# Attention's row maximum: four transposing products and a copy replaced by three DMAs through DRAM

## The chip, the cores and the metric

The kernel runs on one core of a Trainium2 chip. The metric is the device time of one execution in microseconds (us). Three executions of the kernel before took 2077.51, 2079.65 and 2083.77 us, so the median is 2079.65 us. A fourth execution was taken by the profiler; it took 2078.25 us, and from its first to its last instruction (its span) 2076.6 us.

## What is computed

One layer of a hybrid encoder is applied with the same weights to two groups of rows: 2048 rows (`x_prompt`) and 512 rows (`x_sample`), each 1024 wide. Every layer has a softmax attention with 8 query heads over 2 key heads, a gated linear attention in both directions, an output projection, and a gated embedding. What matters here is the softmax:

```python
def one_block(q_blk):
    s = jnp.einsum('bkgqd,btkd->bkgqt', q_blk, k).astype(jnp.float32) * scale
    p = jax.nn.softmax(s, axis=-1)
    return jnp.einsum('bkgqt,btkd->bkgqd', p.astype(v.dtype), v)
```

The queries and keys are scaled so that scores are large: a softmax needs each row's maximum taken off before the exponential.

## The kernel before

`build` calls four stages. `stage1` makes the projections and writes q, k, v and the normalised input to DRAM as fp16 pairs (a high half and a low half). `stage2` does the linear attention. `stage3` does the softmax attention and the gates, and `stage4` the output projection and the embedding. The change is in `stage3`.

`stage3` works through 40 items, in the order of the list `items`. An item is one query head over a chunk of 512 rows. The chunks 0 to 3 are the prompt's; each of their items has 16 tiles of 128 keys. Chunk 4 is the sample's; its items have 4 tiles. So there are 32 long items and 8 short ones. They are counted from 0 here: item 8 is the first head of chunk 1, item 39 the last of all.

For each item there are two passes over the keys:

- **The maxima** (`maxima`). For each block of 128 queries and each group of 512 keys, TensorE makes a product of the high halves (`px`, L809), and VectorE reduces it to one maximum per query (`mx`, L815). A last reduction gives `m`, four numbers on each of 128 partitions. L823 and L824 write -m/4096 as two fp16 numbers, `mt`, 128 x 4 x 2. Then four small products with the identity matrix (L827) turn these onto two partitions of a PSUM tile `pn`, and a copy on ScalarE (L828) puts them as rows 64 and 65 under q's low half, the tile `qb`.
- **The head** (`head`). For each key tile, two products add up the scores: L863 with the high half of q (`qa`), and L864 with `qb`, whose 66 rows are the 64 of q's low half and the two of the maximum. The key tile `kb` holds 4096 in its rows 64 and 65, so that L864 takes the maximum off. ScalarE takes the exponential (L865) and rounds it to fp16 (`phi`, L872); VectorE makes the rest (`plo`, L874). The products L844, L848 and L852 add up the output and the sum.

The maxima of an item are made while the head before it runs: `head` calls `pull` after each exponential, and `pull` advances several generators, among them `all_maxima` by the numbers in `steps`. The list `ahead` says how many steps of the next item's maxima are already taken when a head begins: five for most, six to eighteen near the short items. Other generators run beside it in the same way: `all_gates` (L765 loads x, L769 loads weights, L775 multiplies, L786 loads the linear attention's output), `all_sums` (`normalise`) and `all_stores` (L800 writes the mixed result).

The PSUM pool `ps_x` has two buffers. The maxima's `px`, the `pn` of L827 and the `pn` of `normalise` share them, by one tag.

A scheduler decides the final order of each engine's instructions from the dependencies and priorities, at compile time. At run time each engine runs its own list strictly in order and waits on semaphores. All the DMAs spoken of here are issued by SyncE (SP in the profile), from one such list too: a DMA that waits holds up every DMA behind it. `load_q` (L757, L758) fills `qa` and the first 64 rows of `qb` from DRAM, several items ahead (four buffers of each).

Of the kernel before, what the change touches and what calls it, by code (L numbers as in the profile page):

```python
# [9 lines left out]
F32 = mybir.dt.float32  # L10
F32R = mybir.dt.float32r
F16 = mybir.dt.float16
# [8 lines left out]
P = 128  # L21
# [21 lines left out]
    "wg": [2, 4, P, 2, 8, P],  # L43
    "qs": [NCH, 4, P, 512],
    "og": [NCH, P, 4, 512],
    "mx": [NCH, P, 2, 8, 512],
}

# [663 lines left out]
def stage3(net, s, fin=iter(()), top=None, tail=None):  # L712
    nc, tc, d = net.nc, net.tc, net.d
    with ExitStack() as ctx:
# [88 lines left out]
        def maxima(idx, c, h, q):  # L803
            ks = keys(c)
            n = len(ks)
            mx = net.sm.tile([P, 4, n], F32, name=f"mx{n}")
            def product(ti, b):
                ps = ps_x.tile([P, 512], F32, name="px", tag="px")
                nc.tensor.matmul(ps, lhsT=q[0][:, b * P:(b + 1) * P], rhs=ks[ti][0][:, h // 4],  # L809
                                 start=True, stop=True)  # L810
                return ps

            for b in range(4):
                for i in range(n):
                    nc.vector.tensor_reduce(mx[:, b, i:i + 1], product(i, b), axis=AX.X, op=ALU.max)  # L815
                    yield
            if n > 1:
                m = net.sm.tile([P, 4], F32, name="m")
                nc.vector.tensor_reduce(m, mx, axis=AX.X, op=ALU.max)
            else:  # L820
                m = mx[:, :, 0]
            mt = net.sm.tile([P, 4, 2], F16, name="mt")
            nc.vector.tensor_scalar(mt[:, :, 0], m, -1.0 / M_SCALE, None, ALU.mult)  # L823
            nc.vector.scalar_tensor_tensor(mt[:, :, 1], m, -1.0 / M_SCALE, mt[:, :, 0], ALU.mult, ALU.subtract)  # L824
            ps = ps_n_tile()
            for b in range(4):
                nc.tensor.matmul(ps[0:2, b * P:(b + 1) * P], lhsT=mt[:, b], rhs=net.identh, start=True, stop=True)  # L827
            nc.scalar.copy(q[1][64:66], ps[0:2])  # L828

        def head(ks, h, q, ou, pull, last):  # L830
            kv = h // 4
# [378 lines left out]
def build(tc, d):  # L1210
    with ExitStack() as ctx:
        dram = ctx.enter_context(tc.tile_pool(name="scratch", bufs=1, space=DRAM))
        s = {n: [dram.tile(shape[1:], F16 if n in ("xt", "qt", "kt", "vs", "wg") else F32, name=f"scr_{n}{i}") for i in range(shape[0])]
             for n, shape in SCRATCH.items()}
        net = Net(tc, d, ctx)
        top = ctx.enter_context(ExitStack())
# [25 lines left out]
```

## Time and profile before

| what | value |
| --- | --- |
| median of three executions | 2079.65 us (2077.51 to 2083.77) |
| the profiled execution | 2078.25 us |
| its span | 2076.6 us |
| TensorE (PE) busy | 1982.3 us, 95% |
| VectorE (DVE) busy | 1359.3 us, 65% |
| ScalarE (ACT) busy | 1219.1 us, 59% |
| DMA queue of SP: share of 16 engines | 36.7% |
| share of the chain that ended last | PE 73%, DVE 11%, ACT 9%, DMA 3% |

The granted TensorE clock was 0.986 of full speed in the mean. `stage3` runs from about 600 to 1530 us. A busy time is a sum over instructions; TensorE's products overlap one another, so that one of them shows 380 ns and the next starts about 215 ns after it. Idle time of an engine matters only where another engine waits for it.

### The profile page before, as it was taken

To read this page: it belongs to the slowest core of one execution; us is meant where nothing else is said; L and a number is where in the kernel's file an instruction comes from. 1 tells how busy PE (TensorE), PEld (TensorE's weight loads), DVE (VectorE), ACT (ScalarE), POOL (GpSimd) and SP (SyncE) were. 2 spreads that over 40 slices of the span, in tenths; PEclk is the share of its full clock that TensorE was granted. 3 is DMA by queue.
4 is the path that set the end of the run, shared out by engine and by line. 5 is a ranking of instruction groups with operands and counts; after the bars stand their busy time and mean duration, and the time that the engine had idled before them with its cause. 6 is when DMAs were issued, how large, how long until landed. Compare 5 with 4: busy or idle time off the path is not lost.

```text
span 2076.6 us, 29930 instructions
## 1 busy us (share of the span) xinstructions
PE 1982.3 (95%) x11176; PEld 1221.5 (59%) x11176; DVE 1359.3 (65%) x2295; ACT 1219.1 (59%) x2136; POOL 357.0 (17%) x293
## 2 busy tenths in 40 slices
PE   8999998999879999999999999999989999999998
PEld 6888886556654333333333333333347888888886
DVE  7557655566678889899989988988973222222223
ACT  6645443555559788788878878878873222222222
POOL 2444441000330011011011011100110111111111
PEclk9999999999999999999999999999999999999999
DMA  7745945355775123322213212311235222222220
GB/s 238 221 118 134 222 108 139 112 175 149 219 233 161 49 69 110 92 76 87 66 72 101 96 59 72 109 41 54 69 116 159 86 87 87 86 87 86 82 66 34
DMA packets 253666, 229.81 MB, mean 111 GB/s; under 512 B 99472, under 2 KB 191472, under 8 KB 253520
## 3 DMA queue, kind: packets, MB, share of 16 engines
q1 hardware_dynamic: 253376, 227.37, 36.7%
q8 instruction: 88, 1.44, 0.3%
q0 software_dynamic: 144, 0.52, 0.1%
q14 instruction: 58, 0.48, 0.1%
HBM read 151.89 MB, written 75.96 MB: 110 GB/s over the span
## 4 chain that ended last, share of the span: by engine, by line
PE 73%; DVE 11%; ACT 9%; DMA 3%; issue 3%; POOL 1%; SPq 0%; DVEq 0%; POOLq 0%; ACTq 0%
PE pm L112 37%; PE pg L775 7%; PE po L852 5%; ACT p L865 4%; PE px L809 4%; PE pss L863 3%; DVE plo L874 3%; PE pss L864 3%; PE po L844 3%; PE pp L112 3%; ACT phi L872 2%; DVE mx L815 2%; PE pz L848 2%; DMA scr_ga<-a 1%; PE pt L1127 1%
## 5 line engine op out<-in xcount | busy, mean ns | idle before, releaser
L865 ACT ACTIVATE p<-pss,lnp,qk_scale 128x512 f32<-128x512 f32 x544 | 406.1, 781 | 102.1 <-PE pss L864 89.3
L815 DVE TENSOR_REDUCE mx<-px 128x1 f32<-128x512 f32 x544 | 355.7, 681 | 60.1 <-PE px L809 58.1
L874 DVE TENSOR_TENSOR plo<-p,phi 128x1024 f16<-128x1024 f32 x272 | 341.4, 1257 | 30.0 <-ACT phi L872 27.5
L872 ACT CAST phi<-p 128x1024 f16<-128x1024 f32 x270 | 283.2, 1049 | 5.3 <-PE po L852 0.8
L775 PE MATMUL pg<-xt,wg 128*128 128x512 f16 x960 | 284.3, 378 | 1.4 <-DVE g L780 1.3
L863 PE MATMUL pss<-qa,ka 128*128 128x512 f16 x544 | 206.0, 379 | 10.5 <-ACT p L865 9.4
L809 PE MATMUL px<-ka,qa 128*128 128x512 f16 x544 | 201.0, 381 | 15.7 <-DVE mx L815 9.7
L864 PE MATMUL pss<-qb,kb 66*128 66x512 f16 x544 | 206.0, 382 | 0.3 <-ACT qb L828 0.3
L775 PEld LDWEIGHTS <-wg 128*128 128x128 f16 x960 | 92.9, 97 | 121.7 <-issue 14.8
L1175 DVE SCALAR_TENSOR_TENSOR th<-th,pp 128x512 f32<-128x512 f32 (+1 forms) x41 | 27.7, 676 | 190.0 <-ACT th L1174 190.0
L852 PE MATMUL po<-phi,v 128*128 128x512 f16 x544 | 142.6, 385 | 0.0
L1128 ACT CAST hT<-pt 128x512 fp32r<-128x512 f32 x40 | 23.5, 587 | 170.7 <-PE pt L1127 170.7
L112 PE MATMUL pm<-xt,whl 128*128 128x512 f16 x480 | 107.7, 384 | 1.9 <-ACT l L492 1.9
L112 PE MATMUL pm<-wq_h,xt 128*128 128x512 f32 x320 | 103.9, 405 | 4.5 <-ACT xt L237 4.0
L1174 ACT ACTIVATE th<-pm,rh 128x512 f32<-128x512 f32 (+1 forms) x41 | 27.8, 679 | 134.1 <-PE pm L112 134.1
L898 POOL TENSOR_TENSOR ou<-ou,rs 128x512 f32<-128x512 f32 x20 | 38.2, 1910 | 378.0 <-DVE rs L896 378.0
L112 PE MATMUL pm<-wpg0h,hT 128*128 128x512 f32 x320 | 101.1, 396 | 0.2 <-DVE hT L1129 0.2
L112 PE MATMUL pm<-wo1h,mx 128*128 128x512 f32 x320 | 100.7, 396 | 0.0
L112 PE MATMUL pm<-wo0h,mx 128*128 128x512 f32 x320 | 100.5, 395 | 0.0
L864 PEld LDWEIGHTS <-kb 66*128 66x128 f16 x544 | 52.8, 97 | 79.6 <-issue 24.6
L112 PE MATMUL pm<-wl_h,xt 128*128 128x512 f32 x320 | 99.6, 392 | 0.0
L112 PE MATMUL pm<-wpg1h,hT 128*128 128x512 f32 (+1 forms) x336 | 99.4, 379 | 0.0
(270 smaller groups left out, 3855.6 us busy)
## 6 DMA issues: line engine op xcount, KB each, us to landing
wg<-scr_wg SPq DMA_DIRECT2D x40, 512.0 KB
scr_mx<-hl SPq DMA_DIRECT2D x40, 512.0 KB
mx<-scr_mx SPq DMA_DIRECT2D x20, 1024.0 KB
x<-x_prompt SPq DMA_DIRECT2D x27, 512.0 KB
scr_xt<-xh SPq DMA_DIRECT2D x20, 512.0 KB
xt<-scr_xt SPq DMA_DIRECT2D x20, 512.0 KB
xt<-scr_xt SPq DMA_DIRECT2D x40, 256.0 KB
wstage<-w_in SPq DMA_DIRECT2D x32, 256.0 KB
```

Of the source, the lines that this page charges most:

```text
L112: self.nc.tensor.matmul(out, lhsT=a[k], rhs=b[k], start=first and i == 0, stop=last and i == n - 1)
L775: nc.tensor.matmul(ps, lhsT=w[:, wi, k], rhs=xi, start=i == 0, stop=i == 23)
L809: nc.tensor.matmul(ps, lhsT=q[0][:, b * P:(b + 1) * P], rhs=ks[ti][0][:, h // 4], start=True, stop=True)
L815: nc.vector.tensor_reduce(mx[:, b, i:i + 1], product(i, b), axis=AX.X, op=ALU.max)
L844: nc.tensor.matmul(po[r:r + 32], lhsT=ks[t // 4][2][:, t % 4 + i, kv, g * 32:g * 32 + 32], rhs=lo[:, i], start=t == 2, stop=False)
L848: nc.tensor.matmul(pz[i * 32:i * 32 + 32], lhsT=ones, rhs=(lo, hi)[i // 2][:, i % 2], start=t == 2, stop=t + 4 == n)
L852: e = nc.tensor.matmul(po, lhsT=ks[t // 4][2][:, t % 4 + i, kv], rhs=hi[:, i], start=False, stop=t + i + 1 == n)
L863: nc.tensor.matmul(ps, lhsT=ka[:, kv, cs], rhs=q[0], start=True, stop=False)
L864: nc.tensor.matmul(ps, lhsT=kb[0:66, kv, cs], rhs=q[1][0:66], start=False, stop=True)
L865: e = nc.scalar.activation(p[:, i], ps, AF.Exp, bias=net.lnp, scale=net.qk_scale)
L872: nc.scalar.copy(hi, p)
L874: nc.vector.tensor_tensor(lo, p, hi, ALU.subtract)
```

## The change

`mt` no longer goes through TensorE and ScalarE. SP writes it to DRAM, in a new scratch array `mt` of 40 x 128 x 4 x 2 fp16, one part for each item. Two more DMAs read it back, one for each of the two fp16 halves, straight into rows 64 and 65 of `qb`. Each of these moves 512 single fp16 numbers: from DRAM every eighth number for a block of queries, onto one partition in a row. The four products, the tile `pn` in `maxima` and the copy are gone.

```diff
     "og": [NCH, P, 4, 512],
+    "mt": [40, P, 4, 2],
     "mx": [NCH, P, 2, 8, 512],
...
             nc.vector.scalar_tensor_tensor(mt[:, :, 1], m, -1.0 / M_SCALE, mt[:, :, 0], ALU.mult, ALU.subtract)
-            ps = ps_n_tile()
-            for b in range(4):
-                nc.tensor.matmul(ps[0:2, b * P:(b + 1) * P], lhsT=mt[:, b], rhs=net.identh, start=True, stop=True)
-            nc.scalar.copy(q[1][64:66], ps[0:2])
+            nc.sync.dma_start(out=s["mt"][idx], in_=mt)
+            for l in range(2):
+                nc.sync.dma_start(out=q[1][64 + l:65 + l].rearrange("l (b p) -> l b p", b=4),
+                                  in_=s["mt"][idx][:, :, l:l + 1].rearrange("p b l -> l b p"))
...
-        s = {n: [dram.tile(shape[1:], F16 if n in ("xt", "qt", "kt", "vs", "wg") else F32, name=f"scr_{n}{i}") for i in range(shape[0])]
+        s = {n: [dram.tile(shape[1:], F16 if n in ("xt", "qt", "kt", "vs", "wg", "mt") else F32, name=f"scr_{n}{i}") for i in range(shape[0])]
```

The first added line moves every later line number up by one: what the kernel before has at L864, the changed one has at L865.

The scheduler orders the lists anew. On SP, around the maxima of item 8, there stood before:

```order
L765 DMA xt_9139<-scr_xt_58 128x2x512
L769 DMA wg_9329<-scr_wg_92 128x2048
L757 DMA qa<-scr_qt_66 128x1x512
L758 DMA qb_9385<-scr_qt_66 64x512
L800 DMA scr_mx_104<-hl 256x1x512
L769 DMA wg_9540<-scr_wg_92 128x2048
```

Now there stand:

```order
L766 DMA xt_9152<-scr_xt_58 128x2x512
L770 DMA wg_9339<-scr_wg_92 128x2048
L826 DMA scr_mt_112<-mt 128x8
L758 DMA qa<-scr_qt_66 128x1x512
L759 DMA qb_9392<-scr_qt_66 64x512
L828 DMA qb_8706<-scr_mt_112 1x512x1 x2
L801 DMA scr_mx_144<-hl 256x1x512
L770 DMA wg_9544<-scr_wg_92 128x2048
```

The write of `mt` (L826) and its two reads (L828) came in, with the q load of a later item between them; what stood there before kept its order.

On PE, at the start of item 39, the last head, there stood before:

```order
L827 LDWEIGHTS mt
L827 MATMUL pn<-identh,mt 2x128
L863 LDWEIGHTS ka
L863 MATMUL pss<-qa,ka 128x512
L864 LDWEIGHTS kb
L864 MATMUL pss<-qb_16516,kb 128x512
```

Now there stand:

```order
L853 LDWEIGHTS v
L853 MATMUL po_16526<-phi,v 128x512
L853 LDWEIGHTS v
L853 MATMUL po_16526<-phi,v 128x512
L865 LDWEIGHTS kb
L865 MATMUL pss<-qb_16439,kb 128x512
```

The first product that reads the two rows (`pss<-qb`) moved behind the last output products of the head before it; the products with `mt` are gone.

## Rows read from the trace of the kernel before

**Rows 1.** The page: its first line, and the chain that ended last, by engine.
```profile
span 2076.6 us, 29930 instructions
PE 73%; DVE 11%; ACT 9%; DMA 3%; issue 3%; POOL 1%; SPq 0%; DVEq 0%; POOLq 0%; ACTq 0%
```

**Rows 2.** Busy time in windows: stretch, its us, busy us (instructions) by engine, clock, DMA.
```profile
600.00:1530.00 930.00, 897.68 (x5618) 364.60 (x5619) 823.58 (x1129) 778.61 (x1078) 107.72 (x67) 0.99 0.26 87
```

**Rows 3.** Groups by line, 600 to 1530 us: count | busy us, mean ns | idle before.
```profile
L827 PE MATMUL pn<-identh,mt 128*2 128x128 f16 x156 | 15.0, 218 | 2.7 <-DVE mt L824 2.7
L828 ACT CAST qb<-pn 2x512 f16<-2x512 f32 x39 | 22.4, 573 | 19.8 <-PE pn L827 19.2
```

**Rows 4.** The chain from 1100 to 1160 us: start us, us, what.
```profile
1102.21 0.87 PE pg L775 x4
1103.08 0.55 PE po L844 x8
1103.63 0.43 PE pz L848 x8
```

**Rows 5.** Timeline of PE around item 8's maxima: start us, us, line, operation.
```profile
819.30 0.38 PE L809 MATMUL px<-ka,qa 128*128 128x512 f16 x1
...
820.82 0.38 PE L863 MATMUL pss<-qa,ka 128*128 128x512 f16 x1
821.12 0.38 PE L827 MATMUL pn<-identh,mt 128*2 128x128 f16 x4
821.44 0.39 PE L809 MATMUL px<-ka,qa 128*128 128x512 f16 x1
...
823.35 0.38 PE L864 MATMUL pss<-qb,kb 66*128 66x512 f16 x1
```

**Rows 6.** Timeline of DVE, the same item.
```profile
820.85 0.17 DVE L824 SCALAR_TENSOR_TENSOR mt<-m,mt 128x4 f16<-128x4 f32 x1
```

**Rows 7.** The tile mt: who waited for it (us, times).
```profile
  PE pn L827: 3.9, 6
```

**Rows 8.** Timelines of PE and DVE at item 39, the last.
```profile
1504.92 0.38 PE L809 MATMUL px<-ka,qa 128*128 128x512 f16 x1
...
1511.41 0.81 PE L864 MATMUL pss<-qb,kb 66*128 66x512 f16 x3 [0.34 <-ACT qb L828]
...
1510.16 0.15 DVE L824 SCALAR_TENSOR_TENSOR mt<-m,mt 128x4 f16<-128x4 f32 x1
```

**Rows 9.** Timelines: a store and the DMA that waits for its landing, twice.
```profile
1592.42 1.01 SPq L1188 DMA_DIRECT2D y_prompt<-x  x2
1595.18 0.34 SPq L1057 DMA_DIRECT2D x<-x_prompt  x1
...
922.55 0.56 SPq L800 DMA_DIRECT2D scr_mx<-hl  x1
925.67 0.32 SPq L786 DMA_DIRECT2D hl<-scr_og  x1
```

**Rows 10.** Timelines: a load and the instruction that waits for it, twice.
```profile
0.81 0.45 SPq L93 DMA_DIRECT2D mixn<-mix_norm  x1
3.28 0.17 DVE L132 TENSOR_SCALAR mix<-mixn 128x8 f32<-128x8 f32 x1 [2.25 <-DMA mixn<-mix_norm]
...
593.12 0.55 SPq L757 DMA_DIRECT2D qa<-scr_qt  x1
600.04 0.61 PE L809 MATMUL px<-ka,qa 128*128 128x512 f16 x1 [2.01 <-DMA qa<-scr_qt]
```

**Rows 11.** Waits, 600 to 1530 us: who for whom, us in total, times, longest.
```profile
ACT p L865 <- PE pss L864: 89.3, 94, 4.2
DVE mx L815 <- PE px L809: 56.3, 85, 2.0
PE pss L863 <- ACT p L865: 9.2, 18, 1.7
PE px L809 <- DVE mx L815: 7.6, 16, 1.1
PE po L844 <- DVE plo L874: 7.2, 17, 0.9
```

**Rows 12.** The DMA queue's own waits, 640 to 1530 us.
```profile
SPq L769 <- PE pg L775: 196.1, 20, 17.4
```

## The prediction

> **What bounds the kernel now.** I read the chain that ended last first: TensorE holds 73% of it [rows 1]. All that changes lies in the softmax stage, so I then read the windows there: in the 930 us from 600 to 1530 us PE was busy 897.68 us, DVE 823.58 and ACT 778.61, at 0.99 of the clock and with 0.26 of the DMA engines' time in use [rows 2]. PE binds, but DVE is close behind (89%), and the three work in small steps on each other's results. The waits say in which direction: ACT waited 89.3 us for the score products and DVE 56.3 us for the maxima's products, while PE's larger waits on ACT and DVE sum to 24 us (9.2 + 7.6 + 7.2) [rows 11]. So a microsecond of PE's list is worth nearly a microsecond, and one of ACT's little.
>
> **What is removed.** On PE, 40 groups of four products. Around item 8 the last product before the group starts at 820.82 us and the first after it at 821.44 [rows 5]; without the group the second would start one product later, about 0.215 us (four of them take 0.87 [rows 4]). The group costs 0.62 - 0.215 = 0.405 us, and 40 of them 16.2 us. To this comes what PE waited for `mt` at these products, 3.9 us in 6 waits [rows 7]. Together 20.1 us, all on PE's list. On ACT, a copy of 573 ns and a wait for it, 22.4 + 19.8 us for 39 of the 40 [rows 3]. ACT waits for PE anyway, so I take nothing for it; if ACT's lateness is what holds the products L863 [rows 11], some 5 us could come from there. The maxima also get back a buffer of `ps_x`; that can't be worth more than the 7.6 us that PE waited for a free one [rows 11], and I take nothing.
>
> **What is added.** Three DMAs for each item, 120 in all, on SP's list, and a wait on PE: the first product on `qb` of a head can't start until both rows have landed. Behind that product stands all of PE's list, so the wait stops the gates and the next maxima too. Its size is the length of the chain from `mt` to the rows, less the work that PE still has in front of that product.
>
> **The chain.** The write first. No row shows a 2 KB store; two stores of 256 KB, the second issued about 0.5 us after 1592.42, had landed at 1595.18, so some 2.2 us for that one; a 512 KB store in this stage took 925.67 - 922.55 = 3.1 us [rows 9]. I take 2.2, since ours is smaller than both. The two reads then: the nearest row in kind is the load of `mixn`, which moves 1,024 single 4-byte words and took 3.28 - 0.81 = 2.5 us with nothing else under way; the far one is a load of 128 KB that came in this stage's beginning, 600.04 - 593.12 = 6.9 us [rows 10]. The second read is issued 0.5 us behind the first. So 3.0 to 7.4 us for the pair. I take 5.0, midway: in pieces they are `mixn`, but the two go into the same few places one after the other, and at 21 of the 32 long items the new order has something else between write and reads, a q load as at item 8, or x, weights or a result of 256 KB and more. The chain is 2.2 + 5.0 = 7.2 us, with ends at 5.2 (2.2 + 3.0) and 10.5 (3.1 + 7.4).
>
> What rows say of single numbers is mild: 1,024 of them in 2.5 us [rows 10]. [...]
>
> **The cover.** In the changed order I counted what PE has between the last maxima's product of an item and the first product on its `qb`. A full product counts 1; eight of the 32-wide ones count 2, since they take 0.55 or 0.43 us against 0.22 [rows 4]. In the 32 long items the order before holds 17 to 55 of these (35 in the mean), the new one 23 to 56 (43 in the mean): the scheduler has moved the first use back. At item 8 the order before has 16.6, and they took 823.35 - 819.30 = 4.05 us [rows 5], 0.24 us each. So the new cover is 43 x 0.24 = 10.4 us in the mean. From it goes the time until `mt` is there: 1.7 us at item 8 (819.30 to 821.02) [rows 5, 6], 5.4 at item 39 (1504.92 to 1510.31) [rows 8], 3.9 in the mean of the 32, and 0.3 more in the new order of DVE. What is left for the chain is 6.2 us in the mean: 0.1 at item 39, 4.0 to 8.5 at thirty others, 10.4 at one. The eight short items keep more than 18 us and need none of it.
>
> **The shortfall.** Summed item by item, a chain of 7.2 us comes too late at 25 items, by 41 us in all, 7 of them at item 39; one of 5.2 us at 7 items, by 9 us; one of 10.5 us at all 32, by 139 us. At item 39 nothing follows on PE to be caught up, so its 7 us count in full. Of the other 34 I count 0.6: while PE stands, DVE and ACT work off what they owe, and some of PE's own waits for them (24 us in rows, more in gaps under 0.2 us that rows don't show) go away. Between 0.3 and 1 of it could count. That gives 7 + 0.6 x 34 = 27.4 us.
>
> **Loads behind the new DMAs** cost nothing. SP stops about 2.2 us at each item between write and reads, and behind it wait the loads of weights, x and results. But SP itself stood 196.1 us waiting for PE to give up a weight buffer [rows 12]: a load goes out as soon as its buffer is free, 40 loads in 930 us, so one buffer lasts some 23 us, and a landing of 7 us plus the stop leaves over 10. Were that cover gone, each stop would be 2 us on PE.
>
> **The sum.** 2078.25 - 20.1 + 27.4 = 2085.6 us on the profiled execution, which is 1.4 us below the median of the runs; I say 2086, about 0.3% slower than before. 0.3% (6 us) is about what a measurement of this kernel can tell from no change.
>
> **Rivals.** *The chain is short.* If the loads behave like `mixn` in quiet, it is 5.2 us, the shortfall 9 us, 5 of them at item 39, and 5 + 0.6 x 4 = 7 us are lost: 2078.25 - 20.1 + 7.4 = 2065.6, and with the small gains on ACT and `ps_x` down to some 2060. For it speaks that the scheduler placed the first use where 25 of the 32 covers exceed 5.2 us; against it the DMA traffic of this stage, a quarter of the engines' time. It turns at a chain of about 6.5 us, where loss and gain are equal. *Two-byte pieces are dear.* A load of 512 single numbers then takes as long as the slow load, because each piece has a cost of its own: a chain of 10.5 us is short by 139 us, of which 0.6 or more count, so 2078.25 - 20.1 + 10 + 0.6 x 129 = 2145 or more. [...] Only the 6.9 us row speaks for it [rows 10]; the 1,024 words in 2.5 us speak against. *DVE takes over.* With 89% busy, DVE may set the pace as soon as PE has time to spare; PE's 20 us then buy nothing, and stalls of PE cost nothing either: 2078, give or take 4. Against it stand DVE's 56.3 us of waiting for PE [rows 11]. *It does not do what it says* only in this sense: the products and the copy do go, but their wait comes back as PE's wait for a DMA; that is the forecast itself.
>
> **Chances.** The forecast (chain of 6.2 to 9 us, 2072 to 2105) 0.45: within 0.3% 0.11, slower 0.32, faster 0.02. The short chain 0.31: faster 0.28, within 0.03. DVE takes over 0.13: within 0.11, faster and slower 0.01 each. Dear pieces 0.11: slower. In sum faster 0.31, same 0.25, slower 0.44. The range for 8 in 10 goes from 2061, which leaves out a corner of the short chain, to 2118, which leaves out nearly all of the dear pieces.
>
> **What will show it.** In the changed profile PE's product on `qb` (now L865) should have waits for the DMA `qb<-scr_mt`, some 20 to 25 of them, one to three us each, 35 to 45 us in sum, the longest (6 us or more) at the last item; SP's reads should follow the write by 2 to 2.5 us. Few such waits mean the short chain; over 100 us of them mean dear pieces. If they are there and the time does not move, DVE's idle time in the stage should have shrunk, and DVE bounds. I would be wrong in kind if PE waited for weights or x instead.

## The result

Slower by a fifth: 2501.5 us in the median of four runs (2498.22 to 2504.8) against 2080.76 us for the kernel before beside them (2077.51 to 2083.77), a ratio of 1.202 (95% interval 1.2 to 1.2035). The profiled execution of the changed kernel has a span of 2498.5 us against 2076.6 [rows 1]: 421.9 us more. The forecast of 2086 us and the range up to 2118 are both missed.

The page of the changed kernel: its first line, the busy time by engine, the chain that ended last, and the group of the first product on `qb` (now L865; count | busy us, mean ns | idle before).

```profile
span 2498.5 us, 29774 instructions
...
PE 2042.2 (82%) x11016; PEld 1232.1 (49%) x11016; DVE 1354.7 (54%) x2295; ACT 1199.3 (48%) x2096; POOL 353.9 (14%) x293
...
PE 56%; DMA 25%; DVE 9%; ACT 4%; issue 2%; SPq 1%; POOL 1%; DVEq 0%; POOLq 0%; ACTq 0%
...
L865 PE MATMUL pss<-qb,kb 66*128 66x512 f16 x544 | 230.0, 434 | 363.9 <-DMA qb<-scr_mt 363.9
```

DMA holds 25% of the chain; before it held 3% [rows 1]. The waits of the changed kernel give the same number by name (us in total, times, longest), one line of TensorE and one of SyncE:

```profile
PE pss L865 <- DMA qb<-scr_mt: 363.9, 33, 14.5
...
SPq L828 <- DMA scr_mt<-mt: 105.6, 27, 12.0
```

So TensorE stands 33 times, 11 us each, because the rows are not there. The timeline of one head shows the chain: `mt` is ready on VectorE, the write goes out, the reads follow when it has landed, and TensorE waits for them (start us, us, engine, line, operation, idle before).

```profile
727.00 0.15 DVE L825 SCALAR_TENSOR_TENSOR mt<-m,mt 128x4 f16<-128x4 f32 x1
...
727.18 0.33 SPq L826 DMA_DIRECT2D scr_mt<-mt  x1
729.25 2.03 SPq L828 DMA_DIRECT2D qb<-scr_mt  x2
...
742.98 1.03 PE L865 MATMUL pss<-qb,kb 66*128 66x512 f16 x2 [10.42 <-DMA qb<-scr_mt]
743.81 1.06 PE L776 MATMUL pg<-xt,wg 128*128 128x512 f16 x2
744.66 0.63 PE L864 MATMUL pss<-qa,ka 128*128 128x512 f16 x1
...
749.15 0.38 PE L864 MATMUL pss<-qa,ka 128*128 128x512 f16 x1
```

The write took 2.1 us (727.18 to 729.25). From the first read's issue to TensorE's start it is 13.7 us (729.25 to 742.98), where the prediction had 5.0. By the semaphore events of the whole trace the 80 reads landed 11.8 to 15.8 us after their issue (median 13.6), and the writes 1.4 to 12.4 (median 3.9).

Behind the wait there is a second loss. The product at 744.66 shows 0.63 us, the same product at 749.15 again 0.38. The windows of these stretches (stretch, its us, busy us and count for PE, PEld, DVE, ACT, POOL, granted clock, DMA share, GB/s), and at the end the whole stage:

```profile
733.00:743.00 10.00, 0.02 (x1) 0.02 (x2) 1.45 (x2) 0.00 (x0) 0.00 (x0) 0.72 0.44 59
743.00:746.50 3.50, 3.50 (x15) 1.02 (x19) 0.31 (x1) 2.19 (x4) 0.00 (x0) 0.50 0.11 38
746.50:760.00 13.50, 13.41 (x82) 5.34 (x74) 10.16 (x13) 10.68 (x16) 0.00 (x0) 0.96 0.13 40
...
600.00:1950.00 1350.00, 953.37 (x5433) 373.56 (x5434) 818.19 (x1128) 755.01 (x1033) 105.76 (x68) 0.84 0.32 60
```

While TensorE stood idle the granted clock fell from 1.00 (735 to 737 us) to 0.50 of full speed (739 to 741 us), and after the wait, which ended at 742.98, it was still 0.50 from 746 to 747 us and 1.00 again from 748 us on. Over the stage it is 0.84, where it was 0.99 [rows 2]. PE's busy time on the page rose from 1982.3 to 2042.2 us although 160 products are gone; 76 us more for the same work, if these were worth the 16.2 us of the prediction (an estimate: what was measured is the rise of 59.9 us). The account of the 421.9 us is then 363.9 (waits) + 76.1 (slower products) - 16.2 (products removed) = 423.8. That it closes to 2 us says that TensorE's other idle time hardly changed.

### The profile page after: what moved, and what is told of

It is laid out like the page before. It is cut to its first block, busy times and chain, and to the rows that moved or that the text cites. A ratio compares the mean times of both kernels' runs of the same rounds, so it can differ in the third digit from the quotient of the medians.

```text
span 2498.5 us, 29774 instructions
## 1 busy us (share of the span) xinstructions
PE 2042.2 (82%) x11016; PEld 1232.1 (49%) x11016; DVE 1354.7 (54%) x2295; ACT 1199.3 (48%) x2096; POOL 353.9 (14%) x293
## 4 chain that ended last, share of the span: by engine, by line
PE 56%; DMA 25%; DVE 9%; ACT 4%; issue 2%; SPq 1%; POOL 1%; DVEq 0%; POOLq 0%; ACTq 0%
PE pm L113 31%; DMA qb<-scr_mt 19%; PE pg L776 4%; PE pss L865 4%; DMA scr_mt<-mt 4%; DVE plo L875 3%; DVE mx L816 3%; PE pss L864 3%; PE po L853 3%; PE px L810 2%; PE pp L113 2%; PE po L845 2%; ACT p L866 1%; PE pz L849 1%; DMA scr_ga<-a 1%
## 5 line engine op out<-in xcount | busy, mean ns | idle before, releaser
L865 PE MATMUL pss<-qb,kb 66*128 66x512 f16 x544 | 230.0, 434 | 363.9 <-DMA qb<-scr_mt 363.9
L875 DVE TENSOR_TENSOR plo<-p,phi 128x1024 f16<-128x1024 f32 x272 | 338.8, 1247 | 29.0 <-ACT phi L873 27.3
L776 PE MATMUL pg<-xt,wg 128*128 128x512 f16 x960 | 294.9, 397 | 3.1 <-DMA wg<-scr_wg 2.7
L865 PEld LDWEIGHTS <-kb 66*128 66x128 f16 x544 | 55.7, 105 | 452.5 <-DMA qb<-scr_mt 339.9
L810 PE MATMUL px<-ka,qa 128*128 128x512 f16 x544 | 215.1, 408 | 16.6 <-DVE mx L816 9.7
L864 PE MATMUL pss<-qa,ka 128*128 128x512 f16 x544 | 219.9, 406 | 5.1 <-ACT p L866 4.6
L776 PEld LDWEIGHTS <-wg 128*128 128x128 f16 x960 | 96.5, 101 | 135.1 <-issue 30.2
L790 POOL TENSOR_TENSOR g<-hl,g 128x512 f32<-128x512 f32 x20 | 30.4, 1522 | 518.4 <-DVE g L781 356.3
L845 PE MATMUL po<-plo,v 128*32 128x512 f16 x1088 | 88.4, 403 | 16.7 <-DVE plo L875 16.5
L864 PEld LDWEIGHTS <-ka 128*128 128x128 f16 x544 | 56.2, 103 | 90.1 <-issue 38.2
```

What stands on the lines that cost most here:

```text
L776: nc.tensor.matmul(ps, lhsT=w[:, wi, k], rhs=xi, start=i == 0, stop=i == 23)
L845: nc.tensor.matmul(po[r:r + 32], lhsT=ks[t // 4][2][:, t % 4 + i, kv, g * 32:g * 32 + 32], rhs=lo[:, i], start=t == 2, stop=False)
L864: nc.tensor.matmul(ps, lhsT=ka[:, kv, cs], rhs=q[0], start=True, stop=False)
L865: nc.tensor.matmul(ps, lhsT=kb[0:66, kv, cs], rhs=q[1][0:66], start=False, stop=True)
L875: nc.vector.tensor_tensor(lo, p, hi, ALU.subtract)
```

## The experiments

The kernel before was run again beside each group of kernels (medians 2078.3 to 2080.8 us in the timed groups). All ratios are to these.

### Few engines, or the pieces themselves?

The first theory was that the two reads are shared by few DMA engines. `k16` lays the scratch out so that each read is one strided row; the write becomes 512 four-byte pieces for it. (A read's semaphore is updated 5 times in the changed kernel and 16 times in `k16`. I took this for a change in how the engines share the read; how they share it was not shown.) `scatter` puts the transposition into the write, so that the read is made of long runs. `probe` adds single loads at the program's start to the kernel before.

```diff
(k16)
-    "mt": [40, P, 4, 2],
+    "mt": [40, 4, P, 2],
...
-            nc.sync.dma_start(out=s["mt"][idx], in_=mt)
+            nc.sync.dma_start(out=s["mt"][idx].rearrange("b p l -> p b l"), in_=mt)
...
-                nc.sync.dma_start(out=q[1][64 + l:65 + l].rearrange("l (b p) -> l b p", b=4),
-                                  in_=s["mt"][idx][:, :, l:l + 1].rearrange("p b l -> l b p"))
+                nc.sync.dma_start(out=q[1][64 + l:65 + l],
+                                  in_=s["mt"][idx][:, :, l:l + 1].rearrange("b p l -> l (b p)"))
(scatter)
-    "mt": [40, P, 4, 2],
+    "mt": [40, 8, P],
...
-            nc.sync.dma_start(out=s["mt"][idx], in_=mt)
-            for l in range(2):
...
+            nc.sync.dma_start(out=s["mt"][idx].rearrange("r p -> p r"), in_=mt.rearrange("p b l -> p (b l)"))
+            nc.sync.dma_start(out=q[1][64:66].rearrange("l (b p) -> l b p", b=4),
+                              in_=s["mt"][idx].rearrange("(b l) p -> l b p", l=2))
```

> The changed kernel with the scratch laid out as block, query, half, so that each read takes 512 numbers from one flat run (slowest dimension 512 and not 4); the write then has 512 pieces of 4 bytes. Theory A (few engines): the two reads land 4 to 5 us after issue instead of 13, the chain is 6.5 to 8 us, PE's waits for the rows fall from 364 us to 20 to 60, the time is 2070 to 2110. Theory B (one partition) or C (two bytes): reads stay at 12 us or more, the time stays at 2450 or more.

> The changed kernel with the transposition in the write: 1,024 two-byte pieces from 128 partitions to DRAM, then one read of 8 runs of 256 bytes into both rows. Theory A (few engines): the write is spread over all engines and lands in 3 to 4.5 us, the read in 2.2 us, the chain is 5.5 to 7 us, the time 2062 to 2095. Theory B (one partition): the same or faster, since the read has few pieces, 2060 to 2080. Theory C (two bytes dear in themselves): the write takes 12 us or more, the time stays above 2400.

> The kernel before, with a chain of single loads put ahead of all its work, each followed by a VectorE copy that waits for it, each kind twice. All have 512 pieces from DRAM unless said. (1) as the change has it: 2-byte pieces onto one partition, source 4 x 128; (2) the same pieces from one flat run of 512, so that the slowest dimension is 512; (3) as (1) with 4-byte pieces; (4) 2-byte pieces onto 128 partitions; (5) 4-byte pieces onto 128 partitions; (6) 8 runs of 256 bytes onto two partitions; (7) 2-byte pieces, source 4 x 128, onto four partitions. [...] Theory B (one partition: pieces that land in one partition wait for each other): (1), (2), (3) 6 us or more, (7) a quarter of that, (4), (5) 2.5 us. Theory C (two bytes: a 2-byte piece is dear in itself): (1), (2), (4), (7) dear, (3) and (5) 2.5 us. The kernel's time is about 100 us above the kernel before in each case and says nothing.

`k16` took 2609.44 us, ratio 1.254 (1.2523 to 1.2561): worse than the change. `scatter` took 2536.05 us, 1.219 (1.2152 to 1.2229). Their waits, two lines of `k16` and then two of `scatter`:

```profile
PE pss L865 <- DMA qb<-scr_mt: 462.0, 32, 19.2
...
SPq L828 <- DMA scr_mt<-mt: 314.8, 38, 15.7
```

```profile
PE pss L864 <- DMA qb<-scr_mt: 364.3, 31, 14.2
...
SPq L827 <- DMA scr_mt<-mt: 534.9, 39, 16.4
```

In `scatter` SyncE waits 13.7 us in the mean for each write: the price has moved with the small pieces from the reads to the store, and theories A and B, which had this kernel at 2095 us or less, fall. In `k16` the two parts went opposite ways, by the semaphore events: the reads landed after 10.5 us in the median, where the change has 13.6, and the write of 512 small pieces after 9.7 us, where the change has 3.9. Theory A expected reads of 4 to 5 us, theories B and C 12 us or more; neither has the 10.5. So all that the new layout changed in the reads, with 16 updates of the semaphore in place of 5, brought 3.1 of 13.6 us, the smaller part of the price.

In `probe` the scheduler ran most of the loads side by side, so that only pairs on one destination can be read; two stand on VectorE's timeline, the second of the loads of 512 two-byte pieces onto one partition, issued at 49.15 us, and the first of those onto partitions 64 to 67, issued at 63.58:

```profile
55.48 0.28 DVE L1235 COPY row<-row 1x512 f16<-1x512 f16 x1 [0.93 <-DMA row<-cb]
...
70.40 0.19 DVE L1235 COPY row<-row 4x128 f16<-4x128 f16 x1 [6.85 <-DMA row<-c]
```

That is 6.3 and 6.8 us for half of what one head needs. The other forms are measured in `probe2`.

### What a piece costs, and where

`probe2` holds nothing but a chain of transfers, three of each form, each started by VectorE when the one before had landed. A form is one line like these:

```diff
+        for _ in range(3):
+            then(row[64:65, 0:1])
+            nc.sync.dma_start(out=row[64:65], in_=flat2[:, :, 0:1].rearrange("b p l -> l (b p)"))
+        for _ in range(3):
+            then(row4[64:65, 0:1])
+            nc.sync.dma_start(out=row4[64:65], in_=flat4[:, :, 0:1].rearrange("b p l -> l (b p)"))
```

> This kernel leaves the whole computation out and writes zeros: it holds only a chain of transfers, three of each form, each started when the one before it has landed, so that the time from issue to landing of each form is read on its own. Theory 1 (place): small pieces that go to one SBUF partition are finished one after the other, at about 10 ns each, whatever their size. Then 512 two-byte pieces onto one partition take about 6.5 us, 256 about 4 us, 512 four-byte pieces 6.5 us, 512 pieces of 16 bytes about 6.5 us; the same 512 two-byte pieces spread over 128 partitions about 2.5 us and 1,024 of them about 3 us; the pair of reads of the changed kernel 13 us. Theory 2 (size): a piece of two bytes is dear wherever it lands, since it is less than a word. Then 512 of them over 128 partitions take 6.5 us too, 1,024 take 13 us, and 512 four-byte pieces onto one partition about 2.5 us. Theory 3 (count): any 512 pieces take 6.5 us, wherever and of whatever size. The 16 pieces of 64 bytes should take 2 to 2.5 us by all three.

Its timeline of VectorE; the number in brackets is VectorE's idle time from the copy that starts a transfer to its landing, with the issue in it. Where there are three alike, the middle one is shown. In this order: 512 two-byte pieces onto one partition; 256 of them; 512 four-byte pieces onto one partition; 512 two-byte pieces over 128 partitions; 1,024 over 128; 512 onto partitions 0, 32, 64 and 96; 512 onto 16 partitions that are 8 apart; 16 pieces of 64 bytes onto one; the pair of reads of the changed kernel (the third); and, in two rows, a pair of flat reads of 512 two-byte pieces each, onto partitions 64 and 0.

```profile
28.14 0.15 DVE L1244 COPY row<-row 1x1 f16<-1x1 f16 x1 [6.27 <-DMA row<-flat]
...
42.95 0.15 DVE L1244 COPY row<-row 1x1 f16<-1x1 f16 x1 [4.02 <-DMA row<-flat]
...
54.40 0.14 DVE L1244 COPY row<-row 1x1 f32<-1x1 f32 x1 [3.48 <-DMA row<-flat]
...
62.59 0.15 DVE L1244 COPY thin<-thin 1x1 f16<-1x1 f16 x1 [2.12 <-DMA thin<-wide]
...
71.07 0.15 DVE L1244 COPY thin<-thin 1x1 f16<-1x1 f16 x1 [2.93 <-DMA thin<-wide]
...
90.17 0.15 DVE L1244 COPY row<-row 1x1 f16<-1x1 f16 x1 [4.54 <-DMA row<-flat]
...
100.79 0.15 DVE L1244 COPY row<-row 1x1 f16<-1x1 f16 x1 [2.62 <-DMA row<-flat]
...
148.53 0.15 DVE L1244 COPY long<-long 1x1 f16<-1x1 f16 x1 [2.01 <-DMA long<-gap]
...
185.53 0.15 DVE L1294 COPY last<-row 2x1 f16<-2x1 f16 x1 [13.30 <-DMA row<-mt_d]
...
203.10 0.15 DVE L1301 COPY last<-row 1x1 f16<-1x1 f16 x1 [7.21 <-DMA row<-flat]
205.12 0.15 DVE L1302 TENSOR_TENSOR last<-last,row 1x1 f16<-1x1 f16 x1 [1.88 <-DMA row<-flat]
```

All three theories fall as they were put. Neither count nor size alone does it: the same 512 two-byte pieces, spread over all partitions, take 2.1 us, hardly more than 16 pieces (2.0). Place alone does not: four-byte pieces onto one partition take 3.5 us, not 6.3 (pieces of 16 and of 64 bytes took 3.8 to 4.2, but for one transfer that met another load in the queue). For transfers into SBUF it is size and place together. From 256 to 512 pieces the time grows by 2.25 us, 8.8 ns for each two-byte piece; a four-byte piece costs (3.48 - 2.01) / 512 = 2.9 ns. The pair of reads takes 13.3 us with nothing else under way, so what the changed kernel shows is no contention but the price itself. The layout of the source has a lesser share: one read in the change's form took 7.7 us (in the first such pair, whose other read had gone out long before), a flat one 6.3.

The store of `scatter`, 1,024 single two-byte pieces to DRAM, and the small load that waits for it, on SyncE's timeline of `probe2`: 14.5 us. (The write of the changed kernel, 128 pieces of 16 bytes, took 1.4 to 1.5 us in the same way.) This store comes from all 128 partitions, so that the place in SBUF does not account for its price; why small pieces are dear on the way to DRAM stays open.

```profile
242.34 0.37 SPq L1311 DMA_DIRECT2D sc_d<-ms  x1
256.86 0.23 SPq L1312 DMA_DIRECT2D last<-sc_d  x1
```

`probe3` asks what "place" means: the same 512 two-byte pieces onto two, four or eight partitions, chosen differently.

> As probe2 (the whole computation is left out, zeros are written): a chain of transfers of 512 two-byte pieces each, three of each form, one after the other, that differ only in the partitions they land on. The readings of probe2 (1 partition 6.3 us, 4 partitions 32 apart 4.5, 16 adjoining 3.2, 16 that are 8 apart 2.6, 128 partitions 2.1) fit 1.95 us plus 4.35 us divided by a number of places, if four adjoining partitions and the four 32 above them share one place and 64 above lies another. [...] Theory N (the number of partitions, or of the engines that share the work, alone decides): the three pairs alike, the three fours alike, the three eights alike.

Its timeline of VectorE, the middle one of each three: partitions 64 and 65; 64 and 96; 0 and 64; then 64 to 67; 0, 32, 64, 96; 0, 4, 8, 12; then eight that are 16 apart; 64 to 71; eight that are 4 apart.

```profile
30.32 0.15 DVE L1244 COPY row<-row 1x1 f16<-1x1 f16 x1 [7.52 <-DMA row<-flat]
53.22 0.15 DVE L1244 COPY row<-row 1x1 f16<-1x1 f16 x1 [7.46 <-DMA row<-flat]
71.11 0.14 DVE L1244 COPY row<-row 1x1 f16<-1x1 f16 x1 [5.01 <-DMA row<-flat]
89.46 0.15 DVE L1244 COPY row<-row 1x1 f16<-1x1 f16 x1 [6.48 <-DMA row<-flat]
105.44 0.14 DVE L1244 COPY row<-row 1x1 f16<-1x1 f16 x1 [4.57 <-DMA row<-flat]
117.37 0.14 DVE L1244 COPY row<-row 1x1 f16<-1x1 f16 x1 [3.52 <-DMA row<-flat]
127.73 0.14 DVE L1244 COPY row<-row 1x1 f16<-1x1 f16 x1 [3.19 <-DMA row<-flat]
139.93 0.15 DVE L1244 COPY row<-row 1x1 f16<-1x1 f16 x1 [4.14 <-DMA row<-flat]
150.21 0.14 DVE L1244 COPY row<-row 1x1 f16<-1x1 f16 x1 [2.74 <-DMA row<-flat]
```

Theory N falls: the pairs, the fours and the eights are not alike (7.5 and 5.0 us, 3.5 to 6.5, 2.7 to 4.1). The fit with places, 1.95 us and 4.35 us divided by their number, holds in its order everywhere, with sizes up to 1.2 us off. Partition 64 took 7.52 us with 65 and 7.46 with 96, and 0 with 64 took 5.01; 64 to 67 took 6.48, and 64 to 71 4.14. So in these readings four adjoining partitions share a place, and so do those 32 above them; 64 above is another. By the number of such places the middle times are 6.3 to 7.5 us for one, 4.1 to 5.0 for two, 3.2 to 3.5 for four, 2.6 to 2.7 for eight (the 16 partitions of `probe2` that are 8 apart are eight places), 2.1 for all 128 partitions. What such a place is in the hardware was not shown. Rows 64 and 65, the two that the attention's product needs, are one place by their 7.52 us.

The places are not the whole of it. The two flat reads onto partitions 64 and 0, which lie on different places, landed 9.2 us after the first was issued (195.92 to 205.12); were they free of each other, it would be about 6.9 (6.3, and 0.54 for the later issue). What else two such transfers share, no run here shows.

Why a two-byte piece costs three times a four-byte one stays open; no run here looks inside.

### The rows without the pieces

`flat_reads` is the changed kernel with reads of one run of 1,024 bytes each, and `dve_transpose` a way to have the right rows with 32 pieces: VectorE transposes, and four transfers go from SBUF to SBUF. `flat_reads` does not bring the maxima into the rows; the scale in front of the exponential is set to a millionth there, so that it stays finite.

```diff
(flat_reads)
-                nc.sync.dma_start(out=q[1][64 + l:65 + l].rearrange("l (b p) -> l b p", b=4),
-                                  in_=s["mt"][idx][:, :, l:l + 1].rearrange("p b l -> l b p"))
+                nc.sync.dma_start(out=q[1][64 + l:65 + l],
+                                  in_=s["mt"][idx][64 * l:64 * l + 64].rearrange("(o p) b l -> o (p b l)", o=1))
...
(dve_transpose)
+        mt = net.sm.tile([P, 32], F16, name="mt", bufs=1)
+        nc.gpsimd.memset(mt, 0.0)
...
+            nc.vector.tensor_scalar(mt[:, 0:4], m, -1.0 / M_SCALE, None, ALU.mult)
+            nc.vector.scalar_tensor_tensor(mt[:, 4:8], m, -1.0 / M_SCALE, mt[:, 0:4], ALU.mult, ALU.subtract)
+            tr = net.sm.tile([P, 32], F16, name="tr", bufs=1)
+            nc.vector.transpose(tr, mt)
+            for k in range(4):
+                nc.sync.dma_start(out=q[1][64:66].rearrange("l (b k i) -> l b k i", b=4, k=4)[:, :, k],
+                                  in_=tr[32 * k:32 * k + 8])
```

> The changed kernel with one thing altered in its order of work: each read takes 512 numbers as they lie in DRAM, one run of 1,024 bytes, in place of 512 single numbers. The same write, the same two reads, the same waits and the same queue, but two pieces a head in place of 1,024. What lands in the rows is then not the maxima, and the scale in front of the exponential is a millionth, so that it stays finite: the attention's weights are wrong, all work is done. If the pieces are the cause (theory place and size): write some 1.5 to 4 us and reads some 2 us, a chain of 4 to 6 us, near the 6.2 us that TensorE has in the mean: waits of TensorE for the rows 5 to 30 us in all, 2070 to 2100 us. If the trip through DRAM as such, or SyncE's waiting for the write, is the cause: 2185 us or more.

> The changed kernel with the transposition moved: VectorE transposes the eight numbers of each partition in its four 32x32 blocks (one instruction, to be about as long as the 0.1 to 0.2 us of its neighbours on VectorE), and four transfers from SBUF to SBUF bring eight pieces of 64 bytes each under the low half. No trip through DRAM, and 32 pieces in place of 1,024. If the pieces made the loss: the rows are there some 2.5 us after the transposition, inside the 6.2 us that TensorE has before it wants them; waits at its first product on them under 30 us in all, 2058 to 2078 us, the granted clock of the stage back at 0.98 or above. If any transfer put into this place of the queue made it, or SyncE's waiting for the number: four transfers a head cost as much as three, and the time stays above 2200 us.

`flat_reads` took 2112.47 us, 1.015 (1.0133 to 1.017). With nothing changed but the shape of the reads and the constant in the scale, 389 of the 421 us are gone: the pieces are the cause. But it ends above the expected 2100, with 30.2 us of waits in 12 heads.

```profile
PE pss L865 <- DMA qb<-scr_mt: 30.2, 12, 3.6
```

`dve_transpose` took 2079.46 us, ratio 1.000 (0.9991 to 1.0009): the kernel before, to the microsecond. Its wait for the rows, and then the group of the transposition from 600 to 1530 us:

```profile
PE pss L867 <- DMA qb<-tr: 9.1, 8, 1.8
```

```profile
L828 DVE STREAM_TRANSPOSE tr<-mt 128x32 f16<-128x32 f16 x39 | 7.9, 204 | 1.1 <-DMA qb<-tr 0.4
```

The mechanism came as expected, the gain did not. The pages say where it went: against the kernel before, TensorE's busy time falls by 11.2 us (1982.3 to 1971.1), and its idle time rises by 12.4. Of the idle time 9.1 us are for the rows, and 5.7 and 2.6 more for VectorE's `plo` and `mx`, while the 3.9 us for `mt` are gone. That opened the other end of the sum, below.

### What the pieces cost others

`both` keeps the four products and the copy, and brings the rows a second time under rows 66 and 67, where nobody reads them. `ahead14` is the changed kernel with the maxima 14 steps ahead of their head in place of 5 (15 to 22 around the short items), `before_lead14` the kernel before with that lead.

```diff
(both, against the kernel before)
+            nc.sync.dma_start(out=s["mt"][idx], in_=mt)
+            for l in range(2):
+                nc.sync.dma_start(out=q[1][66 + l:67 + l].rearrange("l (b p) -> l b p", b=4),
+                                  in_=s["mt"][idx][:, :, l:l + 1].rearrange("p b l -> l b p"))
(ahead14, before_lead14)
-        ahead = [5] * 8 + [6, 18, 17, 5] * 4 + [5] * 16
+        ahead = [14] * 8 + [15, 22, 22, 14] * 4 + [14] * 16
...
```

> The kernel before, with its four products and its copy kept, and beside them the write and the two reads of the changed kernel, which bring the rows under rows 66 and 67 of the same tile, where nobody reads them. TensorE does not wait for them, so this prices the three transfers as such. Theory A (the loss of the changed kernel is TensorE's own wait for the rows, and the clock that this wait costs): 2075 to 2100 us, granted clock 0.99 in the stage. Theory B (the 1,024 pieces also hold up what is behind them in the queue and in the DMA engines: the loads of qa, hl, wg and xt): 2150 us or more, with waits of TensorE for qa and wg that the kernel before does not have.

> The changed kernel with the maxima taken earlier: they lead by 14 steps instead of 5 when a head begins (15, 22, 22, 14 around the short items), so that the rows have some 22 us instead of 6. Theory of the wait (all of the 420 us is PE standing for the rows, with the lower clock that follows from standing): the waits go, the clock returns to 0.98 or more, and the time is 2058 to 2085, the gain of 20 us on PE being seen or not. Rival (SP's list: the DMAs hold up the loads of weights and x behind them, whatever the lead): the time stays above 2200, and PE waits for weights.

> The kernel before with the longer lead of the run ahead14 (maxima 14 steps ahead of their head, and 15 to 22 in the stretches of the fifth request group) and nothing else. It tells what the lead itself costs or gives: if the lead is free, 2070 to 2095 us, and all of the 149 us that ahead14 is above the kernel before belongs to the transfers; if buffers or the order suffer from it, 2110 us or more, and that share of ahead14 has nothing to do with the rows.

`both` took 2185.84 us, 1.051 (1.0497 to 1.0531): the three transfers cost 106.5 us though TensorE never waits for them. It waits for what is queued behind them; in the kernel before it waited 2.0 us for `qa` [rows 10] and its waits name none for weights.

```profile
PE pg L776 <- DMA wg<-scr_wg: 29.7, 2, 15.1
PE px L810 <- DMA qa<-scr_qt: 24.6, 3, 12.3
```

The window of its stage:

```profile
600.00:1640.00 1040.00, 921.39 (x5625) 369.90 (x5623) 825.77 (x1131) 781.83 (x1080) 108.32 (x68) 0.94 0.47 79
```

Here, too, the clock is lower (0.94), and PE's busy time on the page is 24 us longer (2006.3). Theory B holds. By the semaphore events a load of weights landed 7.5 us after its issue in the median and 16.4 at the longest; in the kernel before it was 3.7 and 8.1. In the changed kernel TensorE waits only 2.7 us for weights and 3.5 for `qa`, although some loads are as late there (up to 15.3 us for weights): the longer wait for the rows seems to hide them.

`ahead14` took 2229.96 us, 1.072 (1.0706 to 1.0742), `before_lead14` 2109.54 us, 1.014 (1.0124 to 1.0161). A lead that covers most of the chain takes back 271 of the 421 us. The theory of the wait alone, which had 2058 to 2085, falls; the rival has the time, though what TensorE waits for is `qa` more than weights (8.0 us). The lead costs 30 us by itself, and what is left, 120 us, is of the size of the 106.5 of `both`; how it divides was not measured. Its two longest waits:

```profile
PE px L810 <- DMA qa<-scr_qt: 64.6, 9, 14.6
PE pss L865 <- DMA qb<-scr_mt: 51.4, 14, 11.0
```

### What the removed group was worth

`no_rows` is the kernel before with the products and the copy taken out and a memset in their place. `unread` has that memset, and beside it the transposition and the four transfers of `dve_transpose`, into rows that nobody reads. `late_products` is the kernel before with its products two steps further behind the maximum. `lead6` and `one_transfer` are two tries to mend `dve_transpose`: one step more lead; and one transfer of eight pieces of 256 bytes in place of four, for three more instructions on VectorE (this run also has one buffer each for `mx` and `m`). `no_rows` and `unread` have the small scale of `flat_reads` too.

```diff
(no_rows, against the kernel before)
-            ps = ps_n_tile()
-            for b in range(4):
-                nc.tensor.matmul(ps[0:2, b * P:(b + 1) * P], lhsT=mt[:, b], rhs=net.identh, start=True, stop=True)
-            nc.scalar.copy(q[1][64:66], ps[0:2])
+            nc.vector.memset(q[1][64:66], 0.0)
(late_products, against the kernel before)
+            for _ in range(2):
+                yield
             ps = ps_n_tile()
...
(one_transfer, against dve_transpose)
+            tr = net.sm.tile([32, P], F16, name="tr", bufs=1)
+            for k in range(4):
+                nc.vector.transpose(tr[:, 32 * k:32 * k + 32], mt[32 * k:32 * k + 32])
+            nc.sync.dma_start(out=q[1][64:66].rearrange("l (b p) -> l b p", b=4), in_=tr[0:8])
```

> The kernel before without the four products and the copy, and with nothing in their place but a memset of the two rows by VectorE (so the rows hold zero, and the scale in front of the exponential is a millionth, so that it stays finite: the attention's weights are wrong, all other work is done). It prices what the group that the change removes is worth where its replacement costs nothing. If the prediction's term is right (some 20 us of products and waits leave the path): 2056 to 2066 us. If VectorE and ScalarE, at 0.89 and 0.84 of the stage, take the place of TensorE at once: 2072 to 2082 us, with more waits for plo and px, and then the run dve_transpose had nothing more to win.

> dve_transpose and no_rows together: the memset of no_rows gives the rows (zero, with the scale a millionth: the attention's weights are wrong, all other work is done), and beside it VectorE transposes the maxima and the four transfers bring them under rows 66 and 67, where nobody reads them. Nothing waits for the maxima. It parts the 36 us that lie between no_rows (2043.75) and dve_transpose (2079.46). If TensorE's dependence on the maxima gives the gain back: 2044 to 2056 us. If the four transfers and the instruction on VectorE do, by what they take from the queue and from VectorE: 2070 to 2080 us.

> The kernel before with its four products and copy put two steps of the planner behind the maximum that they transpose (the lead of the maxima over their head stays as it was, so the products come two steps nearer to it). Its profile before has 15.0 us of weight loads that wait for mt, and 3.9 us of products. If that wait is what no_rows gained over the 20 us of the prediction: these waits near zero and 2062 to 2072 us, below both kernels. If the products' place in the order does not matter, because VectorE's next value is late then: 2074 to 2084 us.

> As dve_transpose, with the maxima one step further ahead of their head (lead 6 in place of 5). If the 9.1 us of waits for the rows are what keeps dve_transpose at the time of the kernel before: these waits near zero, 2066 to 2076 us. If a lead costs by itself as it did in before_lead14 (30 us for nine steps, some 3 us a step): 2076 to 2086 us, no gain.

> As dve_transpose, but VectorE writes its four 32x32 blocks side by side into one tile of 32 partitions, in four instructions (0.06 to 0.2 us each), and a single transfer of eight pieces of 256 bytes takes the place of the four transfers (SyncE issued those in 2.7 us). If the 9.1 us that TensorE waited for the rows in dve_transpose are the limit: these waits under 4 us, 2070 to 2078 us. If VectorE's busy time is: 40 heads x 3 more instructions, 6 to 20 us more of it, 2080 to 2095 us.

`no_rows` took 2043.75 us, 0.982 (0.9802 to 0.9834), below both of its expectations, and `unread` 2046.1 us, 0.985 (0.9833 to 0.9864), within its first one. So the group with all that hangs on it is worth 35.7 us, more than the 20.1 of the prediction, and four transfers and one instruction on VectorE cost 2.4 us in all. The 33 us between `unread` and `dve_transpose` are what it costs that the attention's product depends on the maxima at all, with the order that the scheduler lays for it. The windows of `unread` and of `dve_transpose`, in this order:

```profile
600.00:1530.00 930.00, 898.45 (x5544) 374.46 (x5545) 849.40 (x1228) 763.29 (x1052) 119.38 (x74) 0.99 0.28 90
```

```profile
600.00:1530.00 930.00, 884.01 (x5429) 359.92 (x5430) 824.27 (x1167) 749.22 (x1032) 105.40 (x68) 0.99 0.27 87
```

Freed of it, TensorE is busy 14 us longer in the same 930 us, VectorE 25 us. By the pages of the whole span, TensorE in `dve_transpose` is idle 22 us longer (106.7 against 84.4 us), of which 9.1 us are waits for the rows and 8.1 and 3.6 us longer waits for `plo` and `mx`, and its 11016 products take 12 us more (1971.1 against 1959.1 us), at a granted clock of 0.982 against 0.987. The other scale is not what makes the difference: the exponential takes 781 and 779 ns in the mean, `plo` 1259 and 1247, the first score product 382 and 379. One thing is not parted: the scheduler lays another order of TensorE's list when the dependence is gone, and the 33 us are the price of both.

`late_products` took 2104.26 us, 1.012 (1.0107 to 1.0141): both expectations missed, 26 us above the kernel before. The waits for `mt` did not go: 17.8 us of the weight loads in 20 waits (before 15.0 in 23) and 8.7 us of the products (before 3.9). The rows now come two steps nearer to the head that wants them; whether that is the cause was not measured. `lead6` took 2081.09 us (0.9987 to 1.001), with 13.3 us of waits for the rows where they were to vanish: a lead of one step more brought nothing. `one_transfer` took 2084.17 us (1.0009 to 1.0028), its waits still 9.0 us, and VectorE 21 us busier in the stage: its second expectation, though its fewer buffers are not parted from it. No version that computes the right rows beats the kernel before.

## Why the prediction was wrong

**What bounds the stage** was right: TensorE's list sets the time, and a wait at the first product on `qb` stops everything.

**The failed step is the price of the pair of reads**: "I take 5.0, midway", between 3.0 and 7.4. It is 13.3 us in quiet and 13.7 in the stage. Both ends came from rows that lacked what makes the price. `mixn` [rows 10] has the same 1,024 pieces, but of four bytes and spread over the partitions (nor was it quite alone: a load of x was issued at 1.32 us, behind it); `probe2` shows that 1,024 two-byte pieces spread out take 2.9 us as well, so the likeness in number, on which the choice rested, counts for nothing. The slow load [rows 10] has no small pieces at all, so that 7.4 was no upper end. The sentence that "the two go into the same few places one after the other" named the cause and put no price on it, and there was no row for one: with no row of many small pieces onto one place, the upper end was open and the range should have said so. The mechanism was right, the size was not: with the medians of the trace, 3.9 us for the write and 13.6 for the reads, the prediction's own count gives 17.5 - 6.2 = 11.3 us at each of the 32 long items, 362 us, and the trace has 363.9. Of these the factor 0.6, with the last item in full, would have kept some 220, and the sum would have been about 2280 us. So two steps failed: the price of the reads, and the factor below.

**The write** at 2.2 us fits the head shown (2.1); in quiet it is less (1.4 to 1.5), in the stage more (median 3.9).

**The cover** of 6.2 us held: at the head shown `mt` is written at 727.15, the rows are there at 742.98, and TensorE waited 10.42 of these 15.8 us, which leaves 5.4; over the 33 waits the median is 6.7, counted from the last `mt` before each. For a short chain it was a little large: `flat_reads`, with a write of 2.6 and reads of 2.3 us in the median, waits 30.2 us at 12 heads, where the count gave 9 us at 7 heads for 5.2 us.

**The factor 0.6** was a factor of 1.2. I counted that a part of each stall is caught up. In fact 363.9 us of stalls cost about 440 us (the 421.9 and what the removal gave back), since by the clock records of the trace the granted clock is at 0.50 when TensorE starts again after 32 of the 33 stalls, and stays there for 3.2 to 6.8 us (12.5 after the last), which no term of the sum held: about 76 us over 33 stalls, 2.3 us each (the estimate above).

**Loads behind the new DMAs cost nothing** is right for transfers with few pieces (`unread` against `no_rows`, 2.4 us; these have no trip through DRAM) and wrong for these (`both`, 106.5 us).

**The removal** at 20.1 us was of the right order for the products (16.2 of it: PE's busy time falls by 19.7 us in `no_rows`, 1982.3 to 1962.6, and by 11.2 in `dve_transpose`) and too low for the group with all that hangs on it (35.7 us). But the gain could not be cashed in by any of the ways tried here of bringing the rows. `dve_transpose` has a chain of 3.7 us in the median, from the end of the transposition to the last landing. That is shorter than the 5.2 us of the first rival, which was to give 2065.6, and it took 2079.46. So the branch with a chance of 0.31 would probably have been wrong by some 14 us had its condition come true: most of what can be won lies in the dependence on the maxima and the order that goes with it, not in the 160 products.

**The rivals.** "Two-byte pieces are dear" is what happened, with its mechanism, its sign and its mark in the profile ("over 100 us of them mean dear pieces": 363.9). Its 2145 "or more" took 10.5 us for the chain; with the stalls that the trace shows and the slower products the same working gives 2078.25 - 20.1 + 363.9 + 76.1 = 2498, against 2500.16 of the profiled execution. That is an account after the fact and no check of the 76.1, which was itself taken from the busy times. Its chance of 0.11 was too low: one row spoke against it, and that row was not like it. "DVE takes over" did not decide: with the same work on VectorE, and a memset more, `unread` runs 33 us shorter than `dve_transpose`.

## What to carry to other kernels

Price a DMA with single elements by where they land and how small they are, not by their number alone: 512 two-byte pieces cost 2.1 us over all partitions and 6.3 to 7.5 us onto partitions that share one place, and 1,024 a head also delayed what was queued behind them (`both`). If a row must be turned, turn it on an engine first, so that the transfer has runs of 64 bytes: here that took the loss away (`dve_transpose`, 2079.46 us), without a gain. And a stall on TensorE can cost more than its length, since the work after it starts at the lower clock: here at 0.50 after 32 of 33, an estimated 2.3 us on top of each 11.

## What was not expected of the hardware

- The cost of a two-byte piece at one place, 8.8 ns, and its fall with the number of places, as if the pieces queued there; the layout with 16 semaphore updates in place of 5 helped little (`k16`, reads of 10.5 us in place of 13.6).
- A four-byte piece at the same place at 2.9 ns, a third.
- 1,024 two-byte pieces stored to DRAM: 14.5 us, 128 pieces of 16 bytes: 1.4 to 1.5 us.
- VectorE turned eight numbers of each of 128 partitions, in four 32x32 blocks, in one instruction of 204 ns, about as long as its neighbours on VectorE.
